# One step of a hybrid trunk on one core: adaLN weights, input and parameters laid out ahead of the launch, mean squares by products with ones

## Chip, cores and metric

The kernel runs on one core of a Trainium2 chip. The metric is the device time of one execution in microseconds (us). The engines are TensorE (PE, its weight loads PEld), VectorE (DVE), ScalarE (ACT), GpSimd (POOL) and SyncE (SP, which here only issues DMAs).

## The reference

One layer of a trunk with shared weights works on two groups of tokens, 128 context tokens and 256 latent tokens, of width 2048. Cut to what matters:

```python
mod = (jax.nn.silu(cond) @ p['w_mod'] + p['b_mod'])[:, None, :]      # cond: one vector for each group
sh1, sc1, g1, sh2, sc2, g2 = jnp.split(mod, 6, axis=-1)              # 6 x 2048
h = _rmsnorm(x, p['ln1_g']) * (1 + sc1) + sh1                        # x * rsqrt(mean(x*x) + EPS) * g
z = h @ p['w_in']                                                    # 2048 -> 5120
q, k, v, cva, cvg, lx, lg = jnp.split(z, IN_SPLITS, axis=-1)
...                                                                  # attention, convolution, RG-LRU -> mix
x = x + g1 * (mix @ p['w_out'])
h = _rmsnorm(x, p['ln2_g']) * (1 + sc2) + sh2
u = _dwconv(h @ p['ffn_up'], ...)                                    # gated FFN, width 5632
x = x + g2 * ((jax.nn.silu(ug) * uv) @ p['ffn_down'])
return x, k, v, h_last                                               # new keys, values, LRU states of the context
```

All numbers are float32. The large products are made of three products of float32r halves (hi and lo).

## The kernel before

All 384 tokens are the moving columns of the products (T = 384), and the 2048 input features are 16 k tiles of 128 partitions. Each weight chunk of up to 128x1024 is loaded by SP (raw), ACT writes its hi part (whi, L150) and DVE the rest (wlo, L152), and PE makes three products for each weight block (mm3, L163 to L165).

The start goes as follows. setup loads the parameter rows and turns them with PE into columns (to_cols, L190, L192). in_proj loads X as rows of tokens (L498, L500), takes the sums of squares with accumulating instructions on ACT and DVE (L513, L511), and has GpSimd raise the mean to the power -0.5 (rstd, L474: three columns, one for each tile of 128 tokens). DVE scales X by it (L516). Meanwhile mod_pair multiplies silu(c) with the columns of w_mod that belong to the first k tile (L294): a piece of w_mod is 128x1024 numbers, four k tiles of both shift and scale, loaded by two DMAs (L284). The result is copied (M, L354), turned by PE (modt, L357), and the columns of shift and scale are put into MC (L362, L365). Then norm_T turns three 128x128 blocks of X with PE (xtp, L482), ACT applies scale and shift (ht, L486), DVE splits into hh and hl (L488, L489), and the projection products of that k tile can start.

in_proj goes through the k tiles in groups of 1, 1, 2, 4, 4, 4 (GROUPS). While the products of a group run, the adaLN columns of the next are computed ("pair" stream); the last two groups use mod_quad, which gives half of that work to DVE. Columns 3072 to 5119 and four EARLY tiles of the projection are made in this phase; queries, keys and values follow in qkv, with attention, the convolution and the LRU beside them as streams in steps. The later adaLN vectors are made by mod_rows (L377, pieces of 4 x 256 columns) and mod_rows_dve (L397). setup2 makes the softplus of the LRU's parameter with 25 small DVE operations (L225 to L241) and loads what is needed later; setup3 turns the late parameters and the cached keys (ckT, L263). attention turns the new keys of four heads with PE and stores them (L712 to L715); recurrent does the same with the last LRU states (L839 to L842).

The order of instructions on each engine is set when the program is built: a scheduler puts them by priority, and high_priority and issue_after move some. Engines take their instructions in that order. Weight buffers: six raw, nine of the kind that holds w_mod pieces.

Of the kernel before, what the change touches and what calls it, by code (L numbers as in the profile page):

```python
# [8 lines left out]
F32 = mybir.dt.float32  # L9
# [6 lines left out]
P = 128  # L16
# [83 lines left out]
class Trunk:  # L100
# [75 lines left out]
    def load_rows(self, name, eng):  # L176
        r0, n = _PACK[name]
        st = self.slot(P, name + "_st")
        eng.dma_start(st[:n, :], self.I["params"][r0:r0 + n, :])
        return st  # L180

    def load_cols(self, name, eng):

        return self.to_cols(name, self.load_rows(name, eng))

    def to_cols(self, name, st):
        nc = self.nc
        n = _PACK[name][1]
        pt = self.aux_ps()
        nc.tensor.transpose(out=pt[:, :n], in_=st[:n, :], identity=self.ident[:n, :n])  # L190
        out = self.cst.tile([P, n], F32, name=name)
        nc.vector.tensor_copy(out, pt[:, :n])  # L192
        return out
# [24 lines left out]
    def setup2(self):  # L218
        nc, I, cst = self.nc, self.I, self.cst
        self.late = {n: self.load_rows(n, nc.gpsimd) for n in ("cvw", "fcb", "fcw0", "fcw1", "fcw2")}  # L220
# [4 lines left out]
        nc.vector.scalar_tensor_tensor(na, lam, -1.0, lam, ALU.mult, ALU.min)  # L225
# [26 lines left out]
        self.ck = self.misc("ck")  # L252
        nc.gpsimd.dma_start(self.ck, I["cache_k"])

    def setup3(self):
        nc = self.nc
        cols = {n: self.to_cols(n, st) for n, st in self.late.items()}
        self.cvw, self.fcb, self.fcw = cols["cvw"], cols["fcb"], [cols[f"fcw{w}"] for w in range(3)]
        for h4 in range(2):
            pt = self.aux_ps()  # L260
            for j in range(4):
                h = h4 * 4 + j
                nc.tensor.transpose(out=pt[:, j * P:(j + 1) * P], in_=self.ck[:, h * P:(h + 1) * P], identity=self.ident)  # L263
            nc.vector.tensor_copy(self.ckT[:, h4 * 4:h4 * 4 + 4, :], pt.rearrange("p (h d) -> p h d", h=4))


    def mod_pair(self, k0, kt):
# [33 lines left out]
    def mod_quad(self, k0):  # L301
# [9 lines left out]
        for i in range(KT + PLAG):  # L311
            if i < KT:
                v = self.misc("rawm").rearrange("p (v w) -> p v w", v=2)
                for vv in range(2):
                    nc.sync.dma_start(v[:, vv], wm[i * P:(i + 1) * P, vv * D + k0 * P:vv * D + (k0 + kt) * P])
# [51 lines left out]
    def mod_rows(self, vec, pm):  # L367
        nc = self.nc
        wm = self.I["w_mod"][:, vec * D:(vec + 1) * D].rearrange("(k p) (j h c) -> k h p j c", p=P, j=4, h=2)
# [4 lines left out]
        for i in range(n + AHEAD):  # L374
            if i < n:
                raws.append(self.misc("rawm").rearrange("p (j c) -> p j c", j=4))
                nc.sync.dma_start(raws[i], wm[i % KT, i // KT])  # L377
# [99 lines left out]
    def norm_T(self, kt, xs, a, b, ffn):  # L477

        nc = self.nc
        pt = self.aux_ps("xtp")  # L480
        for t in range(3):
            nc.tensor.transpose(out=pt[:, t * P:(t + 1) * P], in_=xs[t], identity=self.ident)  # L482
        t = self.slot(T, "ht")
        hi, lo = self.slot(T, "hh", F32R), self.slot(T, "hl", F32R)
        for c, s0, s1 in SEG:
            nc.scalar.activation(t[:, s0:s1], pt[:, s0:s1], AF.Identity, bias=self.MC[:, b, kt, c:c + 1],  # L486
                                 scale=self.MC[:, a, kt, c:c + 1])
        nc.vector.tensor_copy(hi, t)  # L488
        ins = nc.vector.tensor_tensor(lo, t, hi.bitcast(F32), ALU.subtract)  # L489
        if ffn and kt == HOLD:  # L490
            self.hold = ins
        return hi, lo


    def load_x(self, eng):
        nc, I = self.nc, self.I
        self.X = self.cst.tile([P, 3, D], F32, tag="X", name="X")
        eng.dma_start(self.X[:, 0, :], I["x_prompt"])  # L498
        for t in range(2):
            eng.dma_start(self.X[:, 1 + t, :], I["x_sample"][t * P:(t + 1) * P])  # L500

    def in_proj(self):
        nc, tc = self.nc, self.tc
        self.load_x(nc.sync)
        ssq = self.ssq(4, "ssq1")
        for t in range(3):
            for n in range(4):
                x = self.X[:, t, n * 512:(n + 1) * 512]
                j = self.mm_ps("junk")
                if t == 1:  # L510
                    nc.vector.scalar_tensor_tensor(j, x, 1.0 / D, x, ALU.mult, ALU.mult, accum_out=ssq[:, t, n:n + 1])  # L511
                else:
                    nc.scalar.activation(j, x, AF.Square, scale=RD, accum_out=ssq[:, t, n:n + 1])  # L513
        r = self.rstd(ssq, "rstd1")
        for t in range(3):
# [7 lines left out]
        for g, kt in enumerate(GROUPS):  # L523
# [7 lines left out]
            if g == 3:  # L531
                self.setup3()
# [646 lines left out]
```

## Time and profile before

| | us |
|---|---|
| median of 3 runs | 1766.86 |
| lowest, highest | 1765.52, 1767.41 |
| the profiled execution | 1767.67 |
| its span in the trace | 1765.9 |
| PE busy in the span | 1729.8 |

The span runs from the first to the last instruction that the profile shows; the time of an execution has a little around it. A busy PE is one that has products under way, not one at its peak. The granted clock of TensorE was 0.994 of full speed in the mean.

### The profile page before, as it was taken

The numbers are of one execution on the slowest core, as the hardware profiler recorded it, in microseconds if no ns is written. First come the engines' busy times: TensorE is split into PE (matmuls) and PEld (weight loads), VectorE is DVE, ScalarE is ACT, GpSimd is POOL, SyncE is SP. The second block draws the span as 40 slices with busy tenths as digits, with TensorE's granted clock in tenths as the row PEclk, the third lists the DMA queues.
The fourth block names the chain that finished last, engine by engine and source line by source line (L and its number), as shares of the span: only waits on it lengthen the run. The fifth ranks groups of instructions, "written<-read, shape, count | busy, mean of one in ns | idle before, by whom it ended". The sixth has DMA issues, their size and how long they took to land.

```text
span 1765.9 us, 25396 instructions
## 1 busy us (share of the span) xinstructions
PE 1729.8 (98%) x9977; PEld 1565.4 (89%) x9977; DVE 1156.3 (65%) x1663; ACT 741.1 (42%) x1179; POOL 140.9 (8%) x235
## 2 busy tenths in 40 slices
PE   6999999999999989999999999999999999999997
PEld 5789987879977889999989899998989899898987
DVE  4599789988797446469554545459754545448467
ACT  5122446775444335444424343342433434333434
POOL 0100101223332000001000000001000000000002
PEclk9999999999999999999999999999999999999999
DMA  9988759899787444348434343447443344644433
GB/s 331 343 276 296 225 166 298 251 293 318 189 252 253 156 179 129 123 133 273 143 120 131 120 132 121 130 143 236 134 126 125 119 132 130 218 148 125 127 121 111
DMA packets 234552, 325.58 MB, mean 184 GB/s; under 512 B 12140, under 2 KB 169812, under 8 KB 233536
## 3 DMA queue, kind: packets, MB, share of 16 engines
q1 hardware_dynamic: 220976, 277.98, 48.2%
q0 software_dynamic: 13344, 45.94, 10.0%
q8 instruction: 78, 1.28, 0.3%
q14 instruction: 42, 0.34, 0.1%
q10 hardware_dynamic: 112, 0.05, 0.0%
HBM read 316.54 MB, written 7.38 MB: 183 GB/s over the span
## 4 chain that ended last, share of the span: by engine, by line
PE 89%; DVE 5%; issue 2%; DMA 2%; ACT 1%; POOL 1%; SPq 0%; DVEq 0%; POOLq 0%; ACTq 0%
PE mmp L163 28%; PE mmp L164 28%; PE mmp L165 28%; PE modp L294 1%; DMA rawm<-w_mod 1%; DVE wlo L152 1%; DVE acc L406 1%; PE modp L382 1%; DMA G<-gate 1%; PE xtp L482 1%; PE modp L328 1%; DVE cacc L736 0%; PE modp L412 0%; PE o L705 0%; PE S L672 0%
## 5 line engine op out<-in xcount | busy, mean ns | idle before, releaser
L152 DVE TENSOR_TENSOR wlo<-raw,whi 128x1024 fp32r<-128x1024 f32 x371 | 451.7, 1222 | 443.5 <-ACT whi L150 439.6
L150 ACT CAST whi<-raw 128x1024 fp32r<-128x1024 f32 x371 | 387.6, 1046 | 663.1 <-PE mmp L164 373.2
L163 PE MATMUL mmp<-hh,whi 128*128 128x384 f32 x1904 | 646.4, 340 | 3.6 <-DVE z L562 2.9
L164 PE MATMUL mmp<-hl,whi 128*128 128x384 f32 x1904 | 644.5, 338 | 0.1
L165 PE MATMUL mmp<-hh,wlo 128*128 128x384 f32 x1904 | 643.5, 338 | 0.0
L163 PEld LDWEIGHTS mmp<-hh,whi 128*128 128x128 f32 x1904 | 358.5, 188 | 12.1 <-DVE z L562 4.9
L165 PEld LDWEIGHTS mmp<-hh,wlo 128*128 128x128 f32 x1904 | 358.1, 188 | 5.2 <-issue 4.0
L164 PEld LDWEIGHTS mmp<-hl,whi 128*128 128x128 f32 x1904 | 358.6, 188 | 3.9 <-issue 2.8
L164 PE MATMUL mmp<-wlo,gh 128*128 128x512 f32 x504 | 198.9, 395 | 0.1
L165 PE MATMUL mmp<-whi,gl 128*128 128x512 f32 x504 | 198.5, 394 | 0.0
L163 PE MATMUL mmp<-whi,gh 128*128 128x512 f32 x504 | 197.9, 394 | 0.0
L406 DVE SCALAR_TENSOR_TENSOR acc<-rawm,cT,acc 128x1024 f32<-128x1024 f32 x120 | 149.1, 1281 | 5.2 <-DMA rawm<-w_mod 5.2
L163 PEld LDWEIGHTS mmp<-whi,gh 128*128 128x128 f32 x504 | 94.7, 188 | 22.8 <-ACT cv L940 0.8
L164 PEld LDWEIGHTS mmp<-wlo,gh 128*128 128x128 f32 x504 | 94.6, 188 | 22.4 <-DVE wlo L152 0.5
L165 PEld LDWEIGHTS mmp<-whi,gl 128*128 128x128 f32 x504 | 94.6, 188 | 22.2
L936 ACT ACTIVATE cv<-mmp,fcb,fcw 128x384 f32<-128x384 f32 x88 | 59.3, 675 | 120.4 <-PE mmp L165 120.4
L944 DVE SCALAR_TENSOR_TENSOR cv<-mmp,fcw,cv 128x381 f32<-128x381 f32 x176 | 97.0, 607 | 0.0
L1074 DVE TENSOR_TENSOR Y<-mmp,Y 128x512 f32<-128x512 f32 x96 | 65.9, 687 | 40.8 <-PE mmp L165 38.4
L397 POOL DMA_DIRECT2D rawm<-w_mod x64 | 35.0, 548 | 629.8 <-PE modp L412 351.6
L736 DVE SCALAR_TENSOR_TENSOR cacc<-cu,cvw,cacc 128x399 f32<-128x399 f32 x120 | 75.5, 632 | 2.2
L562 DVE TENSOR_TENSOR z<-mmp,z 128x384 f32<-128x384 f32 x100 | 53.4, 553 | 30.2 <-PE mmp L165 30.1
L940 ACT ACTIVATE cv<-mmp,cv,fcw 128x1 f32<-128x1 f32 x176 | 52.2, 349 | 1.4
(477 smaller groups left out, 1612.7 us busy)
## 6 DMA issues: line engine op xcount, KB each, us to landing
raw<-ffn_up SPq DMA_DIRECT2D x176, 512.0 KB, 3.5
raw<-ffn_down SPq DMA_DIRECT2D x84, 512.0 KB, 3.6
raw<-w_in SPq DMA_DIRECT2D x72, 512.0 KB, 6.2
rawm<-w_mod SPq DMA_DIRECT2D x128, 256.0 KB, 5.8
rawm<-w_mod SPq DMA_DIRECT2D x64, 512.0 KB, 8.5
rawm<-w_mod POOLq DMA_DIRECT2D x64, 512.0 KB, 5.4
raw<-w_out SPq DMA_DIRECT2D x32, 512.0 KB, 5.0
raw<-w_in SPq DMA_DIRECT2D x14, 256.0 KB, 5.5
```

The source lines that it names most:

```text
L150: nc.scalar.copy(hi, raw)
L152: nc.vector.tensor_tensor(lo, raw, hi.bitcast(F32), ALU.subtract)
L163: mm(out, lhsT=a[0], rhs=b[0], start=start, stop=False)
L164: mm(out, lhsT=a[0], rhs=b[1], start=False, stop=False)
L165: mm(out, lhsT=a[1], rhs=b[0], start=False, stop=stop)
L406: nc.vector.scalar_tensor_tensor(acc[c], raws[m], col, acc[c], ALU.mult, ALU.add)
L562: self.mark = nc.vector.tensor_tensor(self.z[f], pz[:, :T], self.z[f], ALU.add)
L736: nc.vector.scalar_tensor_tensor(acc, u[:, w:w + N], self.cvw[:, 4 * w + c:4 * w + c + 1], acc, ALU.mult, ALU.add)
L936: nc.scalar.activation(t, p, AF.Identity, bias=self.fcb[:, f:f + 1], scale=w[1])
L940: nc.scalar.activation(t[:, d:d + 1], p[:, r:r + 1], AF.Identity, bias=t[:, d:d + 1], scale=w[i])
L944: nc.vector.scalar_tensor_tensor(tv[:, :, d], pv[:, :, s], w[i], tv[:, :, d], ALU.mult, ALU.add)
L1074: nc.vector.tensor_tensor(y, p, y, ALU.add)
```

## The change

The host lays out more ahead of the launch. w_mod comes as 192 pieces of 128x1024 numbers, each exactly what one buffer holds, so that every piece is one DMA with a run of 4 KB for each partition, in mod_pair, mod_quad, mod_rows and mod_rows_dve. x comes once more, transposed (x_T, 128 partitions by 16 k tiles by 384 tokens), and is loaded with four DMAs. The parameters come as columns, the cached keys transposed; new keys and LRU states leave as columns, and the host turns them. So the PE transposes of norm_T in this phase, to_cols, setup3, the new keys and the LRU states are gone; norm_T stays for the FFN.

With features on partitions, the sum of squares of a token lies across partitions. norm_x squares each k tile (ACT and DVE in turn, times 0.25) and adds them with sixteen products by ones512 (1/512), which leaves the mean square of all 384 tokens on every partition. DVE adds EPS, GpSimd raises 384 columns to the power -0.5, and DVE multiplies X by it in five pieces. The softplus chain of setup2 is issued after the first of these pieces. ssq, junk and rstd are no longer used in this phase.

```diff
-        return self.to_cols(name, self.load_rows(name, eng))
+        c0, n = _PACK[name]
+        out = self.cst.tile([P, n], F32, name=name)
+        eng.dma_start(out, self.I["params"][:, c0:c0 + n])
...
-        nc.vector.scalar_tensor_tensor(na, lam, -1.0, lam, ALU.mult, ALU.min)
+        with self.tc.issue_after(self.scaled.ins):
+            nc.vector.scalar_tensor_tensor(na, lam, -1.0, lam, ALU.mult, ALU.min)
...
-        self.ck = self.misc("ck")
-        nc.gpsimd.dma_start(self.ck, I["cache_k"])
-
-    def setup3(self):
...
+        nc.gpsimd.dma_start(self.G[:, 3072:4096], I["cache_k"])
...
-                v = self.misc("rawm").rearrange("p (v k c) -> p v k c", v=2, k=nk)
-                for vv in range(2):
-                    c0 = vv * D + k0 * P
-                    nc.sync.dma_start(v[:, vv], wm[i * nk * P:(i + 1) * nk * P, c0:c0 + kt * P].rearrange("(k p) c -> p k c", p=P))
-                chunks.append(v)
+                v = self.misc("rawm")
+                nc.sync.dma_start(v, wm[4 * k0 + i])
+                chunks.append(v.rearrange("p (v k c) -> p v k c", v=2, k=nk))
...
+    def norm_x(self):
+
+        nc = self.nc
+        X = self.cst.tile([P, KT, T], F32, tag="X", name="X")
+        for k in range(0, KT, 4):
+            nc.sync.dma_start(X[:, k:k + 4], self.I["x_T"][:, k * T:(k + 4) * T])
+
+        pm = self.mm_ps("msq")[:, :T]
+        for k in range(KT):
+            sq = self.slot(T, "xsq")
+            if k % 2:
+                nc.vector.scalar_tensor_tensor(sq, X[:, k], 0.25, X[:, k], ALU.mult, ALU.mult)
+            else:
+                nc.scalar.activation(sq, X[:, k], AF.Square, scale=0.5)
+            nc.tensor.matmul(pm, lhsT=self.ones512, rhs=sq, start=k == 0, stop=k == KT - 1)
+        r = self.slot(T, "rx")
+        nc.vector.tensor_scalar(r, pm, EPS, None, ALU.add)
+        nc.gpsimd.tensor_tensor(r, r, self.nhalf[:, 0:1].broadcast_to([P, T]), ALU.pow)
+        for k, n in ((0, 1), (1, 3), (4, 4), (8, 4), (12, 4)):
+            x = X[:, k:k + n]
+            ins = nc.vector.tensor_tensor(x, x, r.unsqueeze(1).broadcast_to([P, n, T]), ALU.mult)
+            if k == 0:
+                self.scaled = ins
+        return X
...
-                    self.h.append(self.norm_T(k, [self.X[:, t, k * P:(k + 1) * P] for t in range(3)], 1, 0, False))
+                    self.h.append(self.modulate(k, X[:, k], 1, 0)[:2])
...
-            if g == 3:
-                self.setup3()
...
-        if h % 4 == 3:
-            pk = self.aux_ps("pk")
-            for j in range(4):
-                nc.tensor.transpose(out=pk[:, j * P:(j + 1) * P], in_=self.z[8 + h - 3 + j][:, :P], identity=self.ident)
-            kk = self.misc("kk")[:, :512]
-            nc.scalar.copy(kk, pk)
-            nc.gpsimd.dma_start(self.O["new_k"][:, (h - 3) * P:(h + 1) * P], kk)
+        nc.gpsimd.dma_start(self.O["new_k"][hs], k[:, :P])
```

The order on two engines changes at the start. On PE, around the first projection product (L163), before: modp are the adaLN products with their piece rawm, xtp the transposes of X.

```order
L294 MATMUL modp<-rawm,cT 32x128 x32
L357 MATMUL modt<-ident,M 128x64
L482 MATMUL xtp<-ident,X 128x128 x3
L294 MATMUL modp<-rawm,cT 32x128
L163 MATMUL mmp<-hh,whi 128x384 x3
L164 MATMUL mmp<-hl,whi 128x384
L294 MATMUL modp<-rawm,cT 32x128 x8
L165 MATMUL mmp<-hh,wlo 128x384
```

And with the change (line numbers of the changed file; L269 is the former L294, L332 the former L357, msq are the products by ones):

```order
L269 MATMUL modp<-rawm,cT 32x128 x8
L488 MATMUL msq<-xsq,ones_82 128x384
L269 MATMUL modp<-rawm,cT 32x128 x8
L488 MATMUL msq<-xsq,ones_82 128x384
L332 MATMUL modt<-ident,M 128x64
L488 MATMUL msq<-xsq,ones_82 128x384 x2
L269 MATMUL modp<-rawm,cT 32x128 x16
L163 MATMUL mmp<-hh,whi 128x384 x3
L269 MATMUL modp<-rawm,cT 32x128 x8
L163 MATMUL mmp<-hh,whi 128x384 x2
L269 MATMUL modp<-rawm,cT 32x128 x8
L164 MATMUL mmp<-hl,whi 128x384
```

The last two products by ones now stand behind the turn of the first adaLN columns, and sixteen adaLN products of the second k tile, instead of one, stand ahead of the first L163.

On DVE, at the scaling of X, before (L234 to L241 is the end of the softplus chain, MC the adaLN columns, wlo a weight chunk's lo part, hh and hl the split input):

```order
L516 TENSOR_SCALAR X<-X,rstd_131 128x2048 x3
L233 TENSOR_TENSOR acc<-acc,s_655 128x8
L362 TENSOR_TENSOR MC<-modt,bmodc 128x2 x2
L234 TENSOR_SCALAR acc<-acc 128x8
L365 SCALAR_TENSOR_TENSOR MC<-MC,pcol 128x2
L235 TENSOR_TENSOR acc<-acc,ss 128x8
L238 SCALAR_TENSOR_TENSOR sp_679<-acc,na 128x8
L240 TENSOR_SCALAR spm_682<-sp_679 128x8
L241 TENSOR_SCALAR sp_679<-sp_679 128x8
L152 TENSOR_TENSOR wlo<-raw,whi 128x1024
L488 CAST hh<-ht 128x384
L489 TENSOR_TENSOR hl<-ht,hh 128x384
```

And with the change (L490 adds EPS, L494 scales X, L470 and L471 are the former L488 and L489, L152 as before):

```order
L152 TENSOR_TENSOR wlo<-raw,whi 128x1024
L490 TENSOR_SCALAR rx<-msq 128x384
L152 TENSOR_TENSOR wlo<-raw,whi 128x1024
L494 TENSOR_TENSOR X<-X,rx 128x384
L494 TENSOR_TENSOR X<-X,rx 128x1152
L470 CAST hh<-ht 128x384
L494 TENSOR_TENSOR X<-X,rx 128x1536
L471 TENSOR_TENSOR hl<-ht,hh 128x384
L494 TENSOR_TENSOR X<-X,rx 128x1536
L152 TENSOR_TENSOR wlo<-raw,whi 128x512
```

The scaling waits for GpSimd's power (L491, on rx), two weight chunks and two pieces of X stand ahead of hh, and another piece of X ahead of hl; the softplus chain has moved behind this place.

## Rows read from the trace of the kernel before

**Rows 1.** The page, parts 1 and 4: engines, and the chain that ended last.
```profile
PE 1729.8 (98%) x9977; PEld 1565.4 (89%) x9977; DVE 1156.3 (65%) x1663; ACT 741.1 (42%) x1179; POOL 140.9 (8%) x235
...
PE 89%; DVE 5%; issue 2%; DMA 2%; ACT 1%; POOL 1%; SPq 0%; DVEq 0%; POOLq 0%; ACTq 0%
```

**Rows 2.** Windows by stage: us, busy us of each engine, PEclk, DMA share, GB/s.
```profile
24.00:60.00 36.00, 34.36 (x318) 27.95 (x317) 17.74 (x35) 16.32 (x34) 6.88 (x10) 0.97 1.08 362
...
60.00:120.00 60.00, 58.81 (x452) 48.19 (x450) 41.93 (x75) 14.03 (x19) 1.41 (x2) 1.00 0.90 299
...
120.00:240.00 120.00, 119.37 (x845) 112.45 (x846) 100.66 (x166) 39.11 (x54) 9.05 (x18) 0.99 0.77 244
```

**Rows 3.** Timeline from 0: start us, us, engine, line, operation [idle before <-releaser].
```profile
8.08 0.58 ACT L513 ACTIVATE junk<-X 128x512 f32<-128x512 f32 x1
...
9.30 0.70 DVE L511 SCALAR_TENSOR_TENSOR junk<-X 128x512 f32<-128x512 f32 x1 [5.46 <-DMA X<-x_sample]
...
12.88 0.60 PE L294 MATMUL modp<-rawm,cT 128*32 128x128 f32 x2 [9.38 <-DMA rawm<-w_mod]
...
20.25 0.26 ACT L354 COPY M<-modp 64x128 f32<-64x128 f32 x1 [5.34 <-PE modp L294]
...
20.56 0.27 PE L357 MATMUL modt<-ident,M 64*128 64x64 f32 x1 [0.35 <-ACT M L354]
...
23.45 1.33 PE L163 MATMUL mmp<-hh,whi 128*128 128x384 f32 x3 [0.33 <-DVE hh L488]
```

**Rows 4.** Windows at the start, columns as in rows 2.
```profile
4.00:10.00 6.00, 0.00 (x0) 0.00 (x0) 0.70 (x3) 3.15 (x9) 0.00 (x0) 1.00 0.99 412
...
12.00:16.00 4.00, 2.90 (x24) 1.91 (x26) 3.01 (x21) 2.90 (x10) 0.28 (x1) 1.00 1.19 289
```

**Rows 5.** The chain in order of time: start us, us, what.
```profile
29.25 1.00 PE modp L294 x16
...
87.89 1.15 PE xtp L482 x9
...
100.94 0.44 PE auxp L263 x4
...
188.75 0.66 PE xtp L482 x6
...
385.31 0.67 PE lnm L747 x2
```

**Rows 6.** Groups by line and form up to 60 us: busy us, mean ns.
```profile
L562 DVE TENSOR_TENSOR z<-mmp,z 128x384 f32<-128x384 f32 x16 | 8.6, 554 | 4.1 <-PE mmp L165 4.1
...
L152 DVE TENSOR_TENSOR wlo<-raw,whi 128x1024 fp32r<-128x1024 f32 x6 | 7.3, 1223 | 4.9 <-ACT whi L150 4.9
...
L488 DVE CAST hh<-ht 128x384 fp32r<-128x384 f32 x4 | 1.4, 354 | 1.5 <-ACT ht L486 1.5
...
L233 DVE TENSOR_TENSOR acc<-acc,s 128x8 f32<-128x8 f32 x7 | 1.2, 167 | 0.2
...
L226 ACT ACT_TABLE_LOAD x1 | 1.3, 1283 | 0.0
```

**Rows 7.** Groups of GpSimd by line and form, whole span: busy us, mean ns.
```profile
L1015 POOL TENSOR_TENSOR Y<-Y,raw 128x512 f32<-128x512 f32 x6 | 8.7, 1452 | 203.5 <-ACT mmp L851 203.4
...
L474 POOL TENSOR_TENSOR rstd<-rstd,nhalf 128x1 f32<-128x1 f32 x6 | 3.3, 551 | 77.7 <-DVE rstd L473 77.7
...
L247 POOL MEMSET attn<- 128x2048 f32 x1 | 1.8, 1805 | 0.0
...
L1039 POOL TENSOR_TENSOR Y<-Y,raw 128x640 f32<-128x640 f32 x1 | 1.6, 1590 | 0.9 <-ACT Y L1037 0.9
...
L474 POOL TENSOR_TENSOR rstd<-rstd,nhalf 128x3 f32<-128x3 f32 x1 | 0.9, 876 | 13.7 <-DVE rstd L473 13.7
```

**Rows 8.** Timeline of TensorE about its idle times, columns as in rows 3.
```profile
59.51 0.45 PE L163 MATMUL mmp<-hh,whi 128*128 128x384 f32 x1 [1.07 <-DVE z L562]
...
120.63 0.45 PE L163 MATMUL mmp<-hh,whi 128*128 128x384 f32 x1 [1.82 <-DVE z L562]
```

More of the change, by code (lines that the diff above doesn't have):

```diff
@@ L219, in setup2 @@
         nc, I, cst = self.nc, self.I, self.cst
-        self.late = {n: self.load_rows(n, nc.gpsimd) for n in ("cvw", "fcb", "fcw0", "fcw1", "fcw2")}
+        self.cvw, self.fcb, *self.fcw = (self.load_cols(n, nc.gpsimd) for n in ("cvw", "fcb", "fcw0", "fcw1", "fcw2"))
         tmp = lambda n: self.mp.tile([P, 8], F32, tag="sp8", bufs=6, name=n)
@@ L312, in mod_quad @@
             if i < KT:
-                v = self.misc("rawm").rearrange("p (v w) -> p v w", v=2)
-                for vv in range(2):
-                    nc.sync.dma_start(v[:, vv], wm[i * P:(i + 1) * P, vv * D + k0 * P:vv * D + (k0 + kt) * P])
+                v = self.misc("rawm")
+                nc.sync.dma_start(v, wm[4 * k0 + i])
+                v = v.rearrange("p (v w) -> p v w", v=2)
                 chunks.append(v)
@@ L368, in mod_rows @@
         nc = self.nc
-        wm = self.I["w_mod"][:, vec * D:(vec + 1) * D].rearrange("(k p) (j h c) -> k h p j c", p=P, j=4, h=2)
+        wm = self.I["w_mod"]
         raws = []
@@ L495, in load_x @@
[L495 to L500, printed above, removed]
+        return hi, lo, nc.vector.tensor_tensor(lo, t, hi.bitcast(F32), ALU.subtract)
+    def norm_x(self):
+        nc = self.nc
+        X = self.cst.tile([P, KT, T], F32, tag="X", name="X")
[18 more added lines that the diff above has]
+        return X
@@ L514, in in_proj @@
-        r = self.rstd(ssq, "rstd1")
-        for t in range(3):
-            nc.vector.tensor_scalar(self.X[:, t], self.X[:, t], r[:, t:t + 1], None, ALU.mult)
+        X = self.norm_x()
         self.z = {}
@@ L1164, in build, with _mod_pieces @@
         trunk_kernel(tc, I, O)
+def _mod_pieces(w):
+    import numpy as np
+    out = np.empty((192, P, 1024), np.float32)
+    k0 = 0
+    for kt in GROUPS:
+        nk = 4 // kt
+        a = w[:, :, :2, k0 * P:(k0 + kt) * P].reshape(KT // nk, nk, P, 2, kt * P)
+        out[4 * k0:4 * (k0 + kt)] = a.transpose(0, 2, 3, 1, 4).reshape(-1, P, 1024)
+        k0 += kt
+    for vec in range(2, 6):
+        a = w[:, :, vec]
+        if vec in (2, 4):
+            a = a.reshape(KT, P, 4, 2, 256).transpose(3, 0, 1, 2, 4)
+        else:
+            a = a.reshape(KT, P, 2, 1024).transpose(2, 0, 1, 3)
+        out[32 * vec:32 * vec + 32] = a.reshape(32, P, 1024)
+    return out
 def kernel(**inputs):
@@ L1177 @@
     r = run_bass_kernel_spmd(nc, [arrays], core_ids=[0])
-    return tuple(r.results[0]["out_" + n].reshape(s) for n, s in zip(_OUTS, _RET))
+    out = {n: r.results[0]["out_" + n] for n in _OUTS}
+    out["new_k"] = out["new_k"].reshape(NH, P, CTX).transpose(2, 0, 1)
+    out["new_lru"] = out["new_lru"].reshape(P, 8).T
+    return tuple(out[n].reshape(s) for n, s in zip(_OUTS, _RET))
```

78 lines of the change are left out of this document (24 added, 54 removed).

## The prediction

> **What bounds the kernel now.** I read the page first, for the busy shares and the chain that ended last [rows 1]: TensorE (PE) is busy 98% of the span and carries 89% of the chain, so only two things can move the time: work taken from PE, and stretches in which PE has nothing to do. Then the stages [rows 2]: PE is busy 34.36 of 36 us from 24 to 60, 58.81 of 60 us from 60 to 120, 119.37 of 120 us from 120 to 240, and as full behind that. The transfers are at their limit up to 60 us only (DMA share 1.08) and have room later (0.77 from 120 to 240). So faster loads are worth something only before about 60 us, and what is taken off PE counts in full behind 24 us. Then the order of time at the start [rows 3]: the first product of the input projection (L163) starts at 23.45. Before it PE waits 9.38 us for the first piece of w_mod, which lands behind the three X transfers; the last product of the first adaLN columns ends at 20.2, M is copied at 20.25, the columns are turned at 20.56, and ht, hh and L163 follow. That stretch is bound by the order of bytes, not by PE: the 512-byte runs of w_mod move at 289 GB/s (12 to 16 us), the 8 KB runs of X at 412 GB/s (4 to 10 us) [rows 4].
>
> **The change part by part.** Terms are against the span, 1765.9 us; the profiled execution took 1767.67, so 1.77 lie around the span, and the median of the three runs is 0.81 under the execution.
>
> Term A, the start. X is the same 3.15 MB in runs of 6 KB, and by the rate of [rows 4] it is in at about 12 us, as now (the product for the second third of X starts at 9.30, the last third follows 2.6 us later at 412 GB/s) [rows 3]. A piece of w_mod, 0.52 MB, then takes 1.27 us at 412 GB/s instead of 1.81 at 289, so the fourth lands at 17.1. Its eight products take 1.0 us [rows 5], the copy M 0.26 and the turn 0.27: 18.8. The PE order puts the last two of the sixteen mean-square products behind that turn; the nearest row is the product by the same ones, 128x399, two records of together 0.67 [rows 5], so 1.3 us: 20.1. The other fourteen cost nothing, because PE waits there for DMA anyway (9.38 us in one wait alone); without that cover they would be 9.4 us. The squares on DVE and ACT are eight each, nearest rows 0.70 and 0.58 for 512 columns [rows 3], as before, without the read-outs. DVE adds EPS from PSUM in 0.55 (the 128x384 sums of L562 [rows 6]): 20.7. Then GpSimd (POOL) raises 384 columns to -0.5, c us, and DVE scales: its order has X of 384 and of 1152 columns ahead of the cast hh, 0.45 and 1.3 by the 1.22 us of 1024 columns (L152), hh 0.35 [rows 6]. With hand-overs the first L163 starts at 23.2 + c. In the same order a weight chunk's wlo stands ahead of the first scaling; it would bind only if c were under about 1 us.
>
> c decides everything, and no row has it. From below: POOL's product of the same kind on 512 and 640 columns takes 1.45 and 1.59 us, which is 2.8 and 2.5 ns a column; 384 columns at 2.5 on top of the 0.55 of a one-column pow give 1.5 us. From above: the one pow of 3 columns took 0.876, the six of 1 column 0.551 [rows 7]; if those 0.163 us a column held on, 384 columns would take 0.55 + 383 x 0.163 = 63 us. By operation the upper row is nearer, by width the lower. I take 4 us: every wide row of POOL costs 0.9 to 2.8 ns a column (the memset 1.805 us for 2048), the 3-column pow is the program's first and only one at that width, and two records so narrow don't show how a loop runs when it has hundreds of columns to overlap. This is a choice between ends 40-fold apart, and both ends stay in the range. Term A is 23.2 + 4 - 23.45 = +3.75 (+1.2 to +63).
>
> The Trainium skill (GPSIMD Engine Reference, § 3.1 Elementwise) measured 2.6 cycles an element for a product of two tensors and about 12 where a loop body branches on data; an estimate from it at 1.2 GHz is 0.8 us and 3.8 us for 384 columns. The first agrees with the wide rows here (2.5 ns is 3 cycles); no run shows the second.
>
> Behind this wait the whole projection is queued on PE: sixteen adaLN products of the next group are put ahead of L163, everything else behind it. Of that group's 32 products one stood ahead of L163 until now and 31 behind it; with the change it is sixteen and sixteen. Fifteen products leave the full part of PE, at 1.0 us for eight [rows 5]. Term B: -1.9.
>
> Term C, PE work that goes away behind 24 us. Turning X took three products a k tile; nine of them take 1.15 us in the chain and six 0.66 [rows 5], 0.11 each. 45 come after the first tile: 5.0. The eight of the cached keys take 0.44 for four [rows 5], 0.9; the eight of new_k have the same shape, 0.9; five of the parameters and one of the LRU states, 0.4. Together -7.2. The eviction copies that go with them were on ACT and DVE beside PE. The new stores of keys (eight of 64 KB for two of 256 KB) lie on POOL's queue, where nothing on the chain waits.
>
> Term D, transfers from 24 to 125 us. SP issues half as many w_mod loads and their runs are 4 KB. PE is idle only twice there, 1.07 us at 59.51 and 1.82 at 120.63, both released by a DVE sum [rows 8]. -1, between 0 and -3.
>
> By the Trainium skill (DMA: Bandwidth & Descriptors, Specifications) 512 bytes are enough for line rate. Then longer runs would bring nothing, the fourth piece would land at 19.3, near where it lands now, and the sum would be 2.2 us higher. The rows disagree (289 against 412 GB/s), and I go by the rows.
>
> Term E: the softplus chain for the LRU (25 small DVE operations of about 0.17 us and an ACT table load of 1.28 [rows 6]) ran in the shadow of the start; it now waits for the first scaling and runs inside the first k tile's projection, ahead of hh of the second tile on DVE. The hh that PE waits for may come a little late: +1 (0 to +2).
>
> Sum: 3.75 - 1.9 - 7.2 - 1 + 1 = -5.35. Span 1760.5, execution 1762.3, median 1761.5: **forecast 1761.5 us**, with its own range 1756 (c = 1.5, D = -3, E = 0 give -10.85) to 1763.5 (c = 6).
>
> **Rivals.**
> 1. The pow costs what its two narrow rows say: c = 63, L163 at 86. PE and everything behind it stand still for 60 us; the loads run ahead only until nine w_mod and six weight buffers are full, which can save the few microseconds of term D, not more (-3 more). 63 - 0.25 - 1.9 - 7.2 - 1 + 1 - 3 = about +50.5: 1817.5. For it: same operation, same engine, a difference of 0.33 us between the two widths, the narrow one a mean over six. Against it: only one record of the wider. It decides from c = 13 us on, where the sum passes +0.2%.
> 2. The pow overlaps its columns but is long, 6 to 13 us (16 to 34 ns a column, a tenth to a fifth of the narrow slope): then the lost start pays for the removed PE work, -3.3 to +3.7, 1763.5 to 1770.5.
> 3. The same between 13 and 40 us: 1770.5 to 1797.5.
> 4. c is small, but the transposes were not on the path: the stretch from 60 to 240 us is bound by loads, and C is lost. Against it the DMA shares of 0.90 and 0.77 with PE at 98 and 99% [rows 2]. It would give 1766.5 to 1769, and is counted with rival 2.
>
> **How the numbers follow.** Forecast 0.43, rivals 2 and 4 0.17, rival 3 0.10, rival 1 0.30. A measurement of this kernel tells about 0.2% (3.5 us) from no change, so faster is 0.43, same 0.17, slower 0.40: the likeliest single case is the faster one, though slower holds nearly as much. Cases of both signs hold most of the chance, so the range must reach over rival 1: 1756 to 1820.
>
> **What would show it.** In the profile after: the duration of the one 128x384 POOL product (4 us by the forecast, 63 by rival 1); the start of the first L163 (27 against 86); GB/s of 12 to 20 us near 400; no xtp products before 240 us; PE's busy sum lower by some 7 us but higher by the mean-square products. The forecast is wrong if the pow takes more than 6 us, or if PE's waits from 40 to 60 us (the hh behind the softplus chain) are several microseconds.

## The result, and the profile after

| | before | after |
|---|---|---|
| median | 1767.13 (4 runs) | 1821.63 (4 runs) |
| lowest, highest | 1765.52, 1772.15 | 1819.53, 1823.83 |
| span of the profiled execution | 1765.9 | 1817.8 |
| PE busy in the span | 1729.8 (98%) | 1723.8 (95%) |
| POOL busy in the span | 140.9 | 206.8 |

The ratio is 1.0304, with a 95% interval of 1.0279 to 1.0328: the change made the kernel about 54 us slower. Rival 1 came true, which had 1817.5, and the forecast of 1761.5 did not.

The page after, parts 1 and 4, answers to [rows 1]:

```profile
PE 1723.8 (95%) x9937; PEld 1560.1 (86%) x9937; DVE 1157.9 (64%) x1655; ACT 738.3 (41%) x1168; POOL 206.8 (11%) x240
...
PE 84%; DVE 6%; POOL 4%; issue 3%; DMA 2%; ACT 1%; SPq 0%; DVEq 0%; POOLq 0%; ACTq 0%
PE mmp L163 26%; PE mmp L165 26%; PE mmp L164 26%; POOL rx L491 3%; DMA rawm<-w_mod 1%; DVE acc L381 1%; DVE wlo L152 1%; PE modp L358 1%; PE modp L269 1%; PE msq L488 1%; DVE cacc L713 0%; DMA bias<-na_bias 0%; PE modp L303 0%; DVE acc L297 0%; POOL bias L632 0%
```

PE has less work than before (6.0 us) and still the span is 51.9 us longer, so PE must have stood still. One instruction of GpSimd, L491, holds 3% of the chain. The timeline after, at the same place as [rows 3] (start us, us, engine, line, operation [idle before <-releaser]):

```profile
6.39 8.82 PE L488 MATMUL msq<-xsq,ones 128*128 128x384 f32 x20 [6.39 <-DVE xsq L485]
...
22.50 0.27 PE L332 MATMUL modt<-ident,M 64*128 64x64 f32 x1
...
22.70 1.56 PE L488 MATMUL msq<-xsq,ones 128*128 128x384 f32 x4
...
24.30 0.56 DVE L490 TENSOR_SCALAR rx<-msq 128x384 f32<-128x384 f32 x1
...
24.94 62.46 POOL L491 TENSOR_TENSOR rx<-rx,nhalf 128x384 f32<-128x384 f32 x1 [22.91 <-DVE rx L490]
87.44 1.83 DVE L494 TENSOR_TENSOR X<-X,rx 128x384 f32<-128x384 f32 x2 [61.45 <-POOL rx L491]
...
89.18 0.35 DVE L470 CAST hh<-ht 128x384 fp32r<-128x384 f32 x1
...
89.59 1.33 PE L163 MATMUL mmp<-hh,whi 128*128 128x384 f32 x3 [63.46 <-DVE hh L470]
90.84 1.90 PE L269 MATMUL modp<-rawm,cT 128*32 128x128 f32 x16
92.67 0.62 PE L163 MATMUL mmp<-hh,whi 128*128 128x384 f32 x2
93.22 1.07 PE L269 MATMUL modp<-rawm,cT 128*32 128x128 f32 x16
```

The power on 384 columns takes 62.46 us. DVE's first scaling is released by it, and PE has waited 63.46 us when the first projection product starts, at 89.59 instead of 23.45. The windows of the same execution (us, busy us of each engine, PEclk, DMA share, GB/s) show the rest:

```profile
12.00:16.00 4.00, 4.00 (x26) 2.33 (x25) 0.54 (x2) 0.45 (x2) 0.00 (x0) 1.00 1.03 411
24.00:90.00 66.00, 2.54 (x34) 2.08 (x34) 4.55 (x7) 1.50 (x3) 62.46 (x1) 0.55 0.16 64
...
89.50:92.60 3.10, 3.01 (x19) 2.12 (x19) 3.10 (x4) 0.03 (x1) 0.00 (x0) 0.50 0.00 0
92.60:96.00 3.40, 3.40 (x29) 2.56 (x28) 1.72 (x5) 1.12 (x4) 0.00 (x0) 1.00 0.52 166
```

The transfers ran at 411 GB/s from 12 to 16 us, as forecast, and stopped when the buffers were full (64 GB/s in the mean from 24 to 90): SP waits 65.7 us there for the adaLN products of PE that free a w_mod buffer. DVE, which took 4.55 us of the 66, did not compete with GpSimd in this stretch.

Three marks in the timelines follow the difference through the program: the start of the first L163, the end of the sixtieth addition of a projection block into z (L562 of the kernel before; nearly the end of in_proj), and the end of the span. In profiled executions, in us, with the difference to before in brackets:

| | first L163 | 60th z addition | end |
|---|---|---|---|
| before | 23.45 | 154.31 | 1765.9 |
| after | 89.59 (+66.1) | 208.21 (+53.9) | 1817.8 (+51.9) |

So 12.2 us come back between the first product and the end of in_proj. What gives them back is the second question of the experiments. The long wait is not needed for it: from the first L163 to the sixtieth addition the kernel before takes 130.9 us, the changed kernel 118.6, and the version below with a cheap power and float32r mean squares, which starts only 1.75 us later than the kernel before, 117.0.

### The profile page after: what moved, and what is told of

Its sections match the earlier page's. It is cut to its first block, busy times and chain, and to the rows that moved or that the text cites. A ratio compares the mean times of both kernels' runs of the same rounds, so it can differ in the third digit from the quotient of the medians.

```text
span 1817.8 us, 25212 instructions
## 1 busy us (share of the span) xinstructions
PE 1723.8 (95%) x9937; PEld 1560.1 (86%) x9937; DVE 1157.9 (64%) x1655; ACT 738.3 (41%) x1168; POOL 206.8 (11%) x240
## 3 DMA queue, kind: packets, MB, share of 16 engines
q8 instruction: 78, 1.28, 0.3%
## 4 chain that ended last, share of the span: by engine, by line
PE 84%; DVE 6%; POOL 4%; issue 3%; DMA 2%; ACT 1%; SPq 0%; DVEq 0%; POOLq 0%; ACTq 0%
PE mmp L163 26%; PE mmp L165 26%; PE mmp L164 26%; POOL rx L491 3%; DMA rawm<-w_mod 1%; DVE acc L381 1%; DVE wlo L152 1%; PE modp L358 1%; PE modp L269 1%; PE msq L488 1%; DVE cacc L713 0%; DMA bias<-na_bias 0%; PE modp L303 0%; DVE acc L297 0%; POOL bias L632 0%
## 5 line engine op out<-in xcount | busy, mean ns | idle before, releaser
L152 DVE TENSOR_TENSOR wlo<-raw,whi 128x1024 fp32r<-128x1024 f32 x371 | 451.2, 1220 | 441.0 <-ACT whi L150 437.3
L163 PE MATMUL mmp<-hh,whi 128*128 128x384 f32 x1904 | 644.9, 340 | 68.5 <-DVE hh L470 64.3
L163 PEld LDWEIGHTS mmp<-hh,whi 128*128 128x128 f32 x1904 | 357.6, 188 | 76.7 <-DVE hh L470 65.3
L163 PE MATMUL mmp<-whi,gh 128*128 128x512 f32 x504 | 198.1, 394 | 0.0
L163 PEld LDWEIGHTS mmp<-whi,gh 128*128 128x128 f32 x504 | 94.7, 188 | 22.8 <-ACT cv L913 0.8
L491 POOL TENSOR_TENSOR rx<-rx,nhalf 128x384 f32<-128x384 f32 x1 | 62.5, 62462 | 22.9 <-DVE rx L490 22.9
```

The lines of the kernel that those rows point to most:

```text
L152: nc.vector.tensor_tensor(lo, raw, hi.bitcast(F32), ALU.subtract)
L163: mm(out, lhsT=a[0], rhs=b[0], start=start, stop=False)
L491: nc.gpsimd.tensor_tensor(r, r, self.nhalf[:, 0:1].broadcast_to([P, T]), ALU.pow)
```

## Experiments

Each version is compared with runs of the kernel before that were taken along with it. Apart from the power on half of the columns all differences are below 1%, so only the intervals tell which are clear.

### The power on half of the columns

```diff
-        nc.gpsimd.tensor_tensor(r, r, self.nhalf[:, 0:1].broadcast_to([P, T]), ALU.pow)
+        nc.gpsimd.tensor_tensor(r[:, :192], r[:, :192], self.nhalf[:, 0:1].broadcast_to([P, 192]), ALU.pow)
```

Half of the tokens are then scaled by the mean square itself.

> The changed kernel, with GpSimd's power on 192 of the 384 columns; the other half of the tokens is scaled by mean square + EPS, so part of the normalization is left out. Theory (the loss is the power, at about 0.163 us a column, on the path to the first projection product): the power lasts 0.55 + 191 x 0.163 = 31.7 us, the first L163 starts 31 us sooner, near 58.5, and the time falls by 25 to 31 us, to 1791 to 1797. Rival (the 62 us are a fixed price of the first wide GpSimd instruction, or of its contention with DVE): the power lasts 55 us or more, and the time stays above 1812.

```profile
26.55 31.86 POOL L491 TENSOR_TENSOR rx<-rx,nhalf 128x192 f32<-128x192 f32 x1 [24.52 <-DVE rx L490]
```

Half of the columns, half of the duration: 31.86 for 62.46 us. The median is 1791.5, a ratio of 1.015 (1.0132 to 1.0168), 30.1 us under the full change (27 us by the two ratios), for 30.6 us less of the power. The first L163 starts at 60.59, 29.0 us sooner, where 31 were expected. The price is per column, and nearly all of it is paid by PE.

### The price over the width

This row of powers and products was put into the version with the power on three columns (next section), at the start of the FFN, where GpSimd has nothing to do. It was run once, for the durations alone:

```diff
+        for n in (1, 1, 2, 3, 4, 8, 16, 48, 96):
+            nc.gpsimd.tensor_tensor(pw[:, :n], pw[:, :n], self.nhalf[:, 0:1].broadcast_to([P, n]), ALU.pow)
+        nc.gpsimd.tensor_tensor(pw[:16, :16], pw[:16, :16], self.nhalf[:16, 0:1].broadcast_to([16, 16]), ALU.pow)
+        for n in (3, 96, 384):
+            nc.gpsimd.tensor_tensor(pw[:, :n], pw[:, :n], self.nhalf[:, 0:1].broadcast_to([P, n]), ALU.mult)
```

> The version with the power on three columns, and beside it, on GpSimd while it has nothing to do at the start of the FFN, a row of further powers in one buffer: 1, 1, 2, 3, 4, 8, 16, 48 and 96 columns of 128 partitions, 16 columns of 16 partitions, and products of 3, 96 and 384 columns. They add work that the output doesn't use. Theory: a power costs 0.163 us a column from the first to the last, 0.39 + 0.163 n: 0.55, 0.88, 1.04, 1.69, 3.0, 8.2 and 16.0 us for 1, 3, 4, 8, 16, 48 and 96 columns, the same 3.0 for 16 partitions, and the product of 384 columns takes near 1 us, so the price is the power's and not the width's. Rival: narrow powers carry a start-up that wide ones spread, and the price of a column moves by more than a tenth between 8 and 96 columns, or falls with fewer partitions.

GpSimd's groups by line and form (busy us, mean ns; L1055 and L1056 are the powers, L1058 the products):

```profile
L1055 POOL TENSOR_TENSOR pw<-pw,nhalf 128x96 f32<-128x96 f32 x1 | 15.6, 15626 | 0.1
...
L1055 POOL TENSOR_TENSOR pw<-pw,nhalf 128x48 f32<-128x48 f32 x1 | 8.0, 7999 | 0.1
...
L1056 POOL TENSOR_TENSOR pw<-pw,nhalf 16x16 f32<-16x16 f32 x1 | 3.7, 3669 | 0.1
...
L1055 POOL TENSOR_TENSOR pw<-pw,nhalf 128x16 f32<-128x16 f32 x1 | 2.9, 2895 | 0.1
...
L1058 POOL TENSOR_TENSOR pw<-pw,nhalf 128x384 f32<-128x384 f32 x1 | 1.7, 1691 | 0.1
L1055 POOL TENSOR_TENSOR pw<-pw,nhalf 128x8 f32<-128x8 f32 x1 | 1.7, 1687 | 0.1
...
L1055 POOL TENSOR_TENSOR pw<-pw,nhalf 128x1 f32<-128x1 f32 x2 | 1.1, 540 | 40.8 <-DVE pw L1053 40.8
...
L1058 POOL TENSOR_TENSOR pw<-pw,nhalf 128x96 f32<-128x96 f32 x1 | 0.3, 347 | 0.1
```

From 8 to 96 columns a power costs (15.626 - 1.687) / 88 = 0.158 us a column, from 96 to 384 (with the row of the changed kernel) 0.163. Below 8 columns one row is off the line, 1.28 us for 4 columns where 1.04 was expected. There is no width from which a column gets cheaper, and fewer partitions don't make it cheaper (3.67 us for 16x16 against 2.90 for 128x16). A product of the same 384 columns takes 1.69 us, more than the 1 us that was expected, but 37 times less than the power. So it is this operation that is dear on GpSimd, not the width; a power on another engine was not run.

### Without a wide power: square root, or three columns

The first version takes the root on ACT and the reciprocal on DVE:

```diff
-        nc.gpsimd.tensor_tensor(r, r, self.nhalf[:, 0:1].broadcast_to([P, T]), ALU.pow)
+        nc.scalar.activation(r, r, AF.Sqrt)
+        nc.vector.reciprocal(r, r)
```

> The changed kernel with the power replaced by a square root on ACT and a reciprocal on DVE, as the convolution module does it: a table load 1.28, 0.52 and 2.55 us, so the first L163 near 31.5 instead of 89.6 (23.45 in the kernel before). Theory (the power alone made the change slower, and the 14 us that came back behind the start are PE work taken away): 1761 to 1765, 0.1 to 0.35% faster than before. Rival (most of what came back was loads that ran ahead in the long wait, and the sixteen mean-square products on PE at the start cost what the transposes saved): 1767 to 1772, the same or slightly slower than before.

The second picks the diagonal of the 128x128 blocks of the mean squares (a number for each token, on its own partition), raises three columns to the power, and spreads them again by a product with ones:

```diff
-        nc.vector.tensor_scalar(r, pm, EPS, None, ALU.add)
-        nc.gpsimd.tensor_tensor(r, r, self.nhalf[:, 0:1].broadcast_to([P, T]), ALU.pow)
...
+        for t in range(3):
+            nc.vector.scalar_tensor_tensor(dg[:, t * P:(t + 1) * P], pm[:, t * P:(t + 1) * P], 1.0, self.ident,
+                                           ALU.mult, ALU.mult, accum_out=rc[:, t:t + 1])
+        nc.vector.tensor_scalar(rc, rc, EPS, None, ALU.add)
+        nc.gpsimd.tensor_tensor(rc, rc, self.nhalf[:, :3], ALU.pow)
+        for t in range(3):
+            nc.vector.tensor_scalar(dg[:, t * P:(t + 1) * P], self.ident, rc[:, t:t + 1], 512.0, ALU.mult, ALU.mult)
+        pr = self.mm_ps("rbc")[:, :T]
+        nc.tensor.matmul(pr, lhsT=self.ones512, rhs=dg, start=True, stop=True)
+        nc.scalar.copy(r, pr)
```

> The changed kernel with the power on three columns: DVE picks the diagonal of the mean-square product for each tile of 128 tokens, GpSimd raises 128x3, and one product by ones spreads diag(r) over the partitions again. About 1.2 + 0.9 + 0.6 + 0.7 + 0.5 = 4 us in the place of 62.5, so the first L163 near 31 and the power at 0.9 us. Theory (price by the column): 1760 to 1764. Rival (the power is slow at this place whatever its width): the first L163 above 60, over 1790.

The timeline of the first:

```profile
24.42 1.28 ACT L491 ACT_TABLE_LOAD   x1
...
25.72 0.52 ACT L491 ACTIVATE rx<-rx 128x384 f32<-128x384 f32 x1
26.38 2.54 DVE L492 RECIPROCAL rx<-rx 128x384 f32<-128x384 f32 x1
...
31.11 0.61 PE L163 MATMUL mmp<-hh,whi 128*128 128x384 f32 x2 [2.76 <-DVE hh L470]
```

And of the second:

```profile
27.29 0.87 POOL L496 TENSOR_TENSOR rc<-rc,nhalf 128x3 f32<-128x3 f32 x1 [25.27 <-DVE rc L495]
...
32.55 0.97 PE L163 MATMUL mmp<-hh,whi 128*128 128x384 f32 x4 [0.83 <-DVE hh L470]
```

The medians are 1760.05, ratio 0.9967 (0.9955 to 0.998), and 1759.35, ratio 0.9969 (0.9957 to 0.998): the whole change without its wide power is some 6 us faster than the kernel before. Between the changed kernel and the second version lie 62.3 us by the medians, 59 by the ratios, and the first L163 is 57.0 us sooner, which is close to the power's 62.46 less the 0.87 of the narrow one and some 3.8 us of steps that stand beside it. Both still start L163 late, in part because the mean squares themselves are late (next).

### Mean squares by float32r products

On top of the three columns, the squares and the ones are written as float32r:

```diff
+        ones_r = self.cst.tile([P, P], F32R, name="ones_r")
+        nc.vector.tensor_copy(ones_r, self.ones512)
...
-            sq = self.slot(T, "xsq")
+            sq = self.slot(T, "xsq", F32R)
...
-            nc.tensor.matmul(pm, lhsT=self.ones512, rhs=sq, start=k == 0, stop=k == KT - 1)
+            nc.tensor.matmul(pm, lhsT=ones_r, rhs=sq, start=k == 0, stop=k == KT - 1)
```

> As the kernel with the power on three columns, and the squares are written as float32r (rounded to it), so that each of the sixteen mean-square products is one pass of 0.17 us instead of 0.64. Theory (with the power gone, the start is bound by these products on PE, which the prediction took as covered by the loads): 7 us less PE at the start, the first L163 3 to 5 us sooner than with float32 squares, 1756 to 1761. Rival (they are covered by the loads, as the prediction has it): the first L163 within 1 us of the kernel with float32 squares, the same time within 1.5 us.

```profile
11.98 1.03 PE L490 MATMUL msq<-xsq,ones_r 128*128 128x384 f32 x4 [0.88 <-ACT xsq L489]
...
14.13 0.87 POOL L498 TENSOR_TENSOR rc<-rc,nhalf 128x3 f32<-128x3 f32 x1 [12.11 <-DVE rc L497]
...
25.20 0.96 PE L163 MATMUL mmp<-hh,whi 128*128 128x384 f32 x4 [2.47 <-DVE hh L470]
```

In plain float32 the sixteen products stand as 32 records of 14.0 us together and run until 24.3 in the changed kernel (14.3 us, until 25.0, in the version above); as float32r they keep up with X, and the last four start at 11.98. The first L163 comes 7.35 us sooner than in the version above, but the median, 1757.68 (ratio 0.9953, 0.9939 to 0.9967), is only 1.7 us lower, and the two intervals overlap: a gain in time is not shown.

### The three parts, each alone in the kernel before

The w_mod layout alone (one DMA a piece in place of two):

```diff
-                v = self.misc("rawm").rearrange("p (v k c) -> p v k c", v=2, k=nk)
-                for vv in range(2):
-                    c0 = vv * D + k0 * P
-                    nc.sync.dma_start(v[:, vv], wm[i * nk * P:(i + 1) * nk * P, c0:c0 + kt * P].rearrange("(k p) c -> p k c", p=P))
...
+                v = self.misc("rawm")
+                nc.sync.dma_start(v, wm[4 * k0 + i])
...
```

> The kernel before with one part of the change alone: w_mod laid out piece by piece, one DMA with runs of 4 KB for each piece. Theory: the start is bound by the 512-byte runs of w_mod, and PE's waits up to about 60 us are for its loads; the first L163 starts 1 to 2 us sooner than 23.45, GB/s of the stretch from 12 to 16 us is near 400 instead of 289, and the time falls by 3 to 6 us. Rival: behind 24 us the loads hide behind PE, so the time changes by less than 1.5 us.

The small layouts alone:

```diff
-        return self.to_cols(name, self.load_rows(name, eng))
...
+        eng.dma_start(out, self.I["params"][:, c0:c0 + n])
...
-                nc.tensor.transpose(out=pk[:, j * P:(j + 1) * P], in_=self.z[8 + h - 3 + j][:, :P], identity=self.ident)
...
+        nc.gpsimd.dma_start(self.O["new_k"][hs], k[:, :P])
...
```

> The kernel before with the small layouts alone (parameters, cached keys, new keys and LRU states as columns; X and w_mod as before). Theory: 22 transposes of 0.11 us leave PE, and the time falls by 1.5 to 3 us, half of it behind 240 us. Rival: they lie in gaps of PE or are paid for by their longer DMAs, and the time changes by less than 1 us.

The transposed X alone, with float32r squares and the power on three columns:

```diff
-                    self.h.append(self.norm_T(k, [self.X[:, t, k * P:(k + 1) * P] for t in range(3)], 1, 0, False))
+                    self.h.append(self.modulate(k, X[:, k], 1, 0)[:2])
...
```

> The kernel before with the transposed X alone: mean squares by products of float32r with ones, a power of 3 columns on GpSimd, w_mod and the small layouts as before. Theory: 45 transposes of 0.11 us leave the full part of PE, 5 us, against 1 to 3 us of a later first L163; the time falls by 3 to 5 us, and the three parts alone add up to the 8 to 13 us of the whole with the same power. Rival: it gains less than 1.5 us and the whole gains because the parts need each other (a shorter PE is only of use when the w_mod loads keep up), so that the three sum to less than 6 us.

| part | median | ratio (95% interval) | first L163 | 60th z addition | end |
|---|---|---|---|---|---|
| w_mod layout | 1757.74 | 0.9953 (0.9937 to 0.9968) | 23.18 | 147.31 | 1757.1 |
| small layouts | 1767.30 | 1.0002 (0.9992 to 1.0012) | 22.75 | 148.77 | 1766.4 |
| transposed X | 1769.20 | 1.0008 (0.9994 to 1.0021) | 29.38 | 149.93 | 1761.7 |

The w_mod layout alone gives what the whole does with a cheap power, and more than the 3 to 6 us expected, though its first L163 moves by 0.27 us and not by 1 to 2. The small layouts are 5.5 us ahead at the end of in_proj, and lose it again behind it; one piece of that is a wait of PE that the kernel before does not have, 2.85 us for ACT at an adaLN product:

```profile
338.39 3.32 PE L357 MATMUL modp<-rawm,cT 128*32 128x256 f32 x32 [2.85 <-ACT V L781]
```

The transposed X starts 5.9 us late, is 4.4 ahead at the end of in_proj, and gains nothing in the median. Its twelve times lie in two groups, four from 1762.5 to 1763.5 and eight from 1769.1 to 1771.0, with the profile from the lower one; why is not known. So the theories for the last two parts fell.

### Long runs without fewer DMAs

The w_mod layout, but with two DMAs a piece as before, of 2 KB runs. In the two traces PE, DVE, ACT and GpSimd take their instructions in exactly the order of the kernel before:

```diff
-                nc.sync.dma_start(v, wm[4 * k0 + i])
+                for vv in range(2):
+                    nc.sync.dma_start(v[:, vv * 512:(vv + 1) * 512], wm[4 * k0 + i][:, vv * 512:(vv + 1) * 512])
...
```

> The kernel before with w_mod laid out piece by piece, but each piece of mod_pair and mod_quad still loaded by two DMAs of half a piece: runs of 2 KB instead of 512 bytes, as many DMAs as before, and the same order of instructions on PE, DVE and ACT as before. Theory (the gain of the w_mod layout, 8.9 us, comes from the transfer rate of long runs): the first L163 near 23.2, PE's wait at 118.5 us shorter, and the time falls by 3 to 6 us. Rival (it comes from the order that follows from one DMA a piece: bursts of 32 adaLN products where before 4 and 28 stood apart): the bursts stay apart, GB/s of 12 to 16 us rises all the same, and the time changes by less than 2 us.

The window and the timeline of the start:

```profile
12.00:16.00 4.00, 2.87 (x24) 2.17 (x26) 3.08 (x20) 3.38 (x10) 0.00 (x0) 1.00 1.05 395
```

```profile
17.11 3.68 DVE L516 TENSOR_SCALAR X<-X,rstd 128x2048 f32<-128x2048 f32 x3 [0.67 <-POOL rstd L474]
...
19.18 0.27 PE L357 MATMUL modt<-ident,M 64*128 64x64 f32 x1 [0.35 <-ACT M L354]
...
20.84 0.33 PE L482 MATMUL xtp<-ident,X 128*128 128x128 f32 x1 [0.87 <-DVE X L516]
...
23.35 0.98 PE L163 MATMUL mmp<-hh,whi 128*128 128x384 f32 x2 [1.85 <-DVE hh L488]
```

The scaling of X on DVE in the kernel before, for comparison:

```profile
16.63 3.68 DVE L516 TENSOR_SCALAR X<-X,rstd 128x2048 f32<-128x2048 f32 x3 [0.67 <-POOL rstd L474]
```

The rate rose from 289 [rows 4] to 395 GB/s, and the adaLN columns are turned at 19.18 instead of 20.56. But the first L163 stays where it was, since DVE scales X until 20.8, and the median is 1763.91, ratio 0.9989 (0.9978 to 1.0001). So of the 8.9 us of the w_mod layout at most 4 come from this rise of the rate, and the rival of the expectation held. The rest comes with one DMA a piece: with the order that follows from it, or with its 4 KB runs, which move at 414 GB/s where these have 395 (not separated). One piece can be seen in the chain of waits. With two DMAs (L293, start us, us, what):

```profile
62.28 0.56 PE modp L293 x4
62.84 0.37 PE mmp L164
63.21 0.18 PE mmp L165
63.38 1.85 PE modp L293 x28
65.24 0.38 PE mmp L163
```

And with one (L292):

```profile
61.58 1.86 PE modp L292 x32
63.44 0.37 PE mmp L164
```

An adaLN product in float32 is two records. With two DMAs the scheduler puts two of sixteen (four of 32 records) ahead of the others. The 28 records take as long as the 32 do, so a split costs the 0.56 us of the four and one more product behind a burst, 0.37 instead of 0.18 us: 0.75 us. The 128 records of this form are busy 11.0 us from 60 to 155 us with two DMAs and 7.9 with one.

A second piece is a wait of PE for a sum of DVE and the clock behind it. Timeline and window with two DMAs:

```profile
120.86 0.45 PE L163 MATMUL mmp<-hh,whi 128*128 128x384 f32 x1 [1.82 <-DVE z L562]
```

```profile
120.00:130.00 10.00, 9.14 (x81) 7.82 (x82) 8.98 (x16) 0.25 (x1) 0.00 (x0) 0.83 0.99 353
```

And with one:

```profile
115.27 0.44 PE L163 MATMUL mmp<-hh,whi 128*128 128x384 f32 x1 [1.27 <-DVE z L560]
```

```profile
114.00:124.00 10.00, 8.73 (x98) 7.39 (x99) 9.61 (x18) 1.05 (x1) 0.00 (x0) 1.00 0.96 332
```

The wait is 0.55 us shorter, and the granted clock stays at full speed (2.4 GHz), where with two DMAs, as in the kernel before, it is 0.83 in the mean of ten us and 0.50, the 1.2 GHz level, from 123 to 125: 17% of ten us, so an estimate of 1.7 us. Together with the 3.1 us of the splits that is some 5.3 of the 7.4 us by which one DMA a piece is ahead of two at the sixtieth addition, in one execution of each. Why the wait is shorter, and what else of the order counts, was not taken apart.

### Two parts together

The w_mod layout with the transposed X:

> The kernel before with the w_mod layout and the transposed X (float32r squares, a power of 3 columns), the small layouts as before. If the parts add up, it is where the w_mod layout alone is (1757.7) plus what X alone measured (+1.5), so 1757 to 1760, and the version with all parts (1757.7) owes nothing to the small layouts. Rival: X needs the faster loads, and the transposes that leave PE count then: 1751 to 1755.

The w_mod layout with the small layouts, X as before:

> The kernel before with the w_mod layout and the small layouts, X as before. If the parts add up: 1757 to 1759, as the w_mod layout alone, since the small layouts alone measured +0.6. Rival: 22 transposes less count once the loads keep up, 1754 to 1756.

| parts | median | ratio (95% interval) | first L163 | 60th z addition | end |
|---|---|---|---|---|---|
| w_mod and X | 1758.42 | 0.9956 (0.9937 to 0.9975) | 25.89 | 144.18 | 1754.9 |
| w_mod and small | 1753.68 | 0.9927 (0.9908 to 0.9946) | 20.80 | 141.78 | 1750.7 |
| all, float32r, 3 columns | 1757.68 | 0.9953 (0.9939 to 0.9967) | 25.20 | 142.21 | 1753.1 |

The version without the transposed X has the lowest median of all and beats both kernels, 11.8 us under the 1765.52 of before in its comparison; it is below both ranges of its expectation (1754 to 1759). The w_mod layout with X came as expected. The parts don't add. The small layouts are worth nothing alone, and some 4 us on top of the w_mod layout (the two intervals overlap a little). One reason is that the wait of 2.85 us above is missing when both are in. The start shows another: alone, w_mod moves the first L163 by 0.27 us and the small layouts by 0.70, together by 2.65. The timelines of the version with both:

```profile
12.51 5.46 PE L267 MATMUL modp<-rawm,cT 128*32 128x128 f32 x64 [12.51 <-ACT junk L486]
15.01 3.68 DVE L489 TENSOR_SCALAR X<-X,rstd 128x2048 f32<-128x2048 f32 x3 [0.99 <-POOL rstd L447]
...
18.41 0.24 PE L330 MATMUL modt<-ident,M 64*128 64x64 f32 x1 [0.44 <-ACT M L327]
...
20.80 0.97 PE L163 MATMUL mmp<-hh,whi 128*128 128x384 f32 x4 [1.67 <-DVE hh L461]
```

Two chains end side by side there, the adaLN columns (loads, PE) and the scaling of X (DVE). With 2 KB runs alone only the first was earlier; here the second is too, 15.01 instead of 17.11: ACT's last sum of squares starts at 13.03 instead of 14.68. That goes with the softplus chain, most of which is done before X lands when the parameters come as columns (DVE is busy 3.42 us from 4 to 10, and 0.23 with 2 KB runs alone); that it is the reason is argued, not shown.

With the transposed X added to this version the median is 4.0 us higher; the intervals overlap a little, so a loss by X is likely but not shown, and there is no sign of a gain. The first L163 moves from 20.80 to 25.20, and at the end of in_proj 4.0 of these 4.4 us are back. PE's busy time does not fall with X, it is 1714.8 us without and 1717.8 with it: the mean squares take what the transposes give.

## Why the prediction was wrong

**The step that failed is the choice of c = 4 us in term A.** Of two ends, 1.5 and 63, the text took one near the lower, arguing that wide rows of GpSimd cost 0.9 to 2.8 ns a column and that two narrow records don't show how a long loop runs. They did show it: 0.55 + 383 x 0.163 = 63 us from [rows 7], 62.46 measured. All wide rows that spoke for the lower end were of other operations. The row of the same operation was the nearest one, and its slope held up to 384 columns, 128 times the width of its wider record. The Trainium skill (GPSIMD Engine Reference, § 3.1 Elementwise) led to the same side: its 12 cycles an element for data-dependent branching make an estimate of 3.8 us, and 0.163 us at the 1.2 GHz of that section's example would be, as an estimate, some 195 cycles. The runs decide; for the product of 384 columns they have 1.69 us, about twice the estimate of 0.8 us from its 2.6 cycles for a tensor_tensor (an add there).

**Term A, the cover of the mean-square products, was mis-sized.** Fourteen of sixteen were to cost nothing because PE waits for DMA anyway, and rx was to be ready at 20.7. It was ready at 24.86: in plain float32 they are 14.0 us of PE records (0.88 a product, where 0.67 was taken), more than the wait of 9.38 us that was to cover them, and they hold up the adaLN products. That is also why rival 1 put the first L163 at 86 and it came at 89.59. As float32r they are done as X lands, and L163 comes 7.35 us sooner; in the median that is 1.7 us, within the noise of the two intervals.

**Rival 1 came out in size too.** It had +62.5 us at the first L163 and +50.5 at the end; measured are +66.1 and +51.9. That the 14.2 us between the two are near its 12.1 is luck in part, since the terms that make up the 12.1 did not hold (below). PE's clock fell as well: it was granted at 0.5, the 1.2 GHz level, while PE stood idle, and eight adaLN products (sixteen records) behind the stall took 1.90 us where a full clock gives 1.07 (the same burst at 93.22, above). It is back at 2.4 GHz from 92.6 on, so this costs one or two microseconds of the 51.9, an estimate from the 3.1 us at half speed.

**Term D had the wrong mechanism and was far too small.** The w_mod layout alone gives 8.9 us, not 1 (0 to 3). The forecast 412 GB/s came (411), but the rate was not what the time hung on: 395 GB/s in the old order gave 1.6 us. That the start is bound by the order of bytes was half of the truth, since the scaling of X, 16.63 to 20.3 in the kernel before, ends beside the turn of the columns at 20.8. The rule of the Trainium skill (DMA: Bandwidth & Descriptors, Specifications), that 512 bytes are enough for line rate, is against the rates here (289 with 512-byte runs, 395 with 2 KB), but what the prediction drew from it, that longer runs bring nothing, was near (1.6 us, 4 at most).

**Term C did not reach the end of the span.** The 45 transposes of X were put at 5.0 us. Between the first L163 and the end of in_proj, X gains 4.0 us when it is added to the best version, 5.8 beside the w_mod layout alone and 10.3 in the kernel before, so the share of the transposes in it is not shown. It is paid for by the start, which the squares, products, diagonal and scaling of a transposed X make later, by 4.4 us in the best version. The other 2.2 us of term C, the small transposes, are 0 alone: PE is ahead by 5.5 us at the end of in_proj and loses it later, 2.85 us of it in the wait for ACT. The premise that what is taken off PE counts in full behind 24 us did not hold: with the small layouts PE's busy time fell by 2.9 us and the median did not fall (ratio 1.0002).

**Terms B and E** were not measured apart. By the order, B's sixteen adaLN products stand ahead of L163; what they are worth is not shown. For E, PE waits 0.83 us for the hh of the second tile in the changed kernel (L163 at 109.59), near the +1 of the forecast; but DVE is done with the softplus chain by then and waits 0.45 us for ACT's ht.

With the price of three columns, 0.87 us, in place of 4, the prediction's sum is 1758.4, and the version with that price ran at 1759.35. That the rest of the sum came out so close is luck: term A had the first L163 at 24.1 where it came at 32.55 (3.8 us of it for the steps that this version has beside the power), term C counted 7.2 us that the parts alone do not give, and term D left out most of what the w_mod layout gives.

## What to carry to other kernels

The price of an operation that the trace has only in a narrow form is extrapolated from that form's own slope, even from two records, before the rows of wider but other operations are asked; and a wide instruction of such an operation in the one place where every engine waits behind it is tried on a few columns first. A statistic that is one number for each token should be raised to a power as one number for each token (three columns), not 128 times over. A layout that turns two DMAs into one also changes the order that a scheduler makes, and the part that changes it least is tried alone: here one of three parts carried most of the gain, one gained only beside it, and one gained nothing.

## What the hardware showed unexpectedly

GpSimd's power costs 0.158 to 0.163 us a column from 8 to 384 columns, and no less for fewer partitions (3.67 us for 16 columns of 16, 2.90 of 128); at 384 columns that is 37 times a product of the same size. Sixteen products of 384 columns with ones are 14.0 us of PE records in float32 and 5.3 in float32r, with waits for X inside the latter. On the other side a reciprocal of 384 columns takes DVE 2.54 us, and a root ACT 0.52 behind a table load of 1.28, so the direct way over two engines costs 4.3 us where GpSimd takes 62.
